# One decoder layer on one core: other PSUM pools, an earlier start of gate/up, read-backs moved into gate/up, and a last quarter in two halves

## The chip, the core and the metric

The kernel runs as one program on one core of a Trainium2 chip. The core has five engines, each with its own in-order instruction queue: TensorE (PE in the rows, its weight loads PEld), VectorE (DVE), ScalarE (ACT), GpSimd (POOL) and SyncE (SP). SP issues nearly all DMA transfers, POOL the accumulating ones. The metric is the time of one execution in microseconds; the kernel before takes 2859.53 us, the median of three runs from 2858.51 to 2861.17.

## What is computed

One layer of a hybrid decoder with 512 tokens and a width of 2048, in float32:

```
u = RMSNorm(h);  p = u @ W_in          # 80 column blocks of 128 for three groups of heads
y = concat(SSD(p), RG_LRU(p), mLSTM(p))  # 2048 + 1024 + 1024 columns
h = h + y @ W_out
g, v = split(RMSNorm(h) @ W_gate_up)   # 2 x 5632 columns
h = h + (silu(g) * v) @ W_down
out = RMSNorm(h)
```

The RG-LRU group (here: LRU) has 8 column blocks. Each block convolves its input over time, multiplies it with two small block-diagonal matrices, takes sigmoids, exponentials and a square root of them, and runs a scan over the tokens.

## The kernel before

Every float32 product with a large weight matrix is made of three fp32r matmuls: both operands are split into a rounded high part and a low part (`hi`, `lo`), and hi x hi, hi x lo and lo x hi are added in PSUM. A weight tile `raw` (128 x 1024) is loaded, ACT copies it to `whi`, DVE subtracts to get `wlo`; three buffers of each are used in turn. Its two halves are the moving operands of 128 x 512 matmuls; the stationary operand is a 128 x 128 piece of an activation tile (`three`, L738 to 743). In the input projection it is the other way round: weights stationary, `u` moving (L144 to 146).

The stages follow each other:

- Input projection with the three groups (L205 to 700). For each block of 128 columns TensorE runs 48 matmuls into a bank `mm` (3 banks), and small matmuls and transposes of the groups, in 5 banks `sm`, are placed between them. `lru(i)` (L429) multiplies the convolved tile `xc` (one buffer) with two matrices into two banks `ps_l` (L447); ACT reads each with a sigmoid (`tr`, `ti`), and a chain on ACT, DVE and POOL ends in a scan and the next block's `xc`. Blocks 6 and 7 come after the last mLSTM head.
- Read-back of the SSD half: `ssd_half` loads 16 tiles `yt`, scales and splits them into `vh`, `vl`.
- Output projection (L728 to 800): the first half of W_out's rows for 4 column blocks, then the second half for 4 column blocks, each 8 weight tiles by 4 token tiles into 4 of 6 banks `ac`. After each block of the second half, h's new tiles `hx` are transposed (`tp`, 2 banks), scaled to `ft` and partly split for gate/up.
- Gate/up (L848 to 920): `seven(j)` for 11 column blocks. It is one step of Strassen's scheme: 7 products ("blocks" 1, 5, 6, 3, 7, 2, 4 in that order) in place of 8, of 48 matmuls each. The weights' sums are made by DMA: `more` issues accumulating transfers on POOL's queue into the tiles `k1` (4 buffers) and `k2` (4). `swiglu` makes the activation, TensorE transposes it, and it is stored to DRAM (`at`).
- Down (L924 to 957): the activations are read back (`ae`), split into a pool of 54 tiles and multiplied with W_down, first the blocks 0 to 5 and then 6 to 10, each for 4 column blocks of 4 token tiles: 88 weight tiles of 24 matmuls, 2112 in all. At the end each of the 4 token tiles is normalised in one DVE instruction of 128 x 2048 and stored.

The order of each engine's instructions is made when the program is built: a scheduler takes the instructions by their place in the code and by when it reckons operands and buffers to be ready, and a pool hands out a buffer when the one before is released. A new PSUM pool without `reuse_waits="tile"` takes the place of the closed pools as a whole; with it, a new tile waits only for the tiles that lay where it lies.

Where tiles lie in a partition of SBUF is fixed at the build, too. The starts of `whi` and `wlo`, of the split activations of the output projection, and of those of gate/up are 224 bytes past a multiple of 256. Those of down's 54 tiles are 96 bytes past one.

Of the kernel before, what the change touches and what calls it, by code (L numbers as in the profile page):

```python
# [15 lines left out]
F32 = mybir.dt.float32  # L16
F32R = mybir.dt.float32r
AF = mybir.ActivationFunctionType
ALU = mybir.AluOpType
# [47 lines left out]
def trunk(tc, A, out):  # L67
# [207 lines left out]
    with tc.tile_pool(name="ssd", bufs=2, side="right", reuse_waits="tile") as sp:  # L275
# [39 lines left out]
        for g in range(NG):  # L315
# [15 lines left out]
            ps = bank("ps_bt")  # L331
# [71 lines left out]
            ps = bank("ps_g")  # L403
# [25 lines left out]
    def lru(i):  # L429
# [315 lines left out]
    def all_tokens(srcs, x):  # L745

        ps = [acc_bank() for _ in range(4)]
        for n, src in enumerate(srcs):
            w = halves(raw_tile(src))
            for j in range(2):  # L750
                for t in range(4):
                    three(ps[t], x(2 * n + j, t), w[j], n + j == 0, n == len(srcs) - 1 and j == 1)
        return ps

    def token_tile(xs):
        return lambda k, t: tuple(v[:, t * P:(t + 1) * P] for v in xs[k])

    with tc.tile_pool(name="wo", bufs=2, reuse_waits="tile") as wo:
# [15 lines left out]

        xs = {}
# [5 lines left out]
        for mb in range(4):  # L781
            cols = slice(mb * T, (mb + 1) * T)
            ps = all_tokens([A["w_out"][1, mb, n] for n in range(8)], token_tile(yb))
            for t in range(4):
# [4 lines left out]
                dve.bn_stats(out=stats[:, t, mb], in_=xt)  # L789
                tp = ps_tp.tile([P, T], F32, name="tp", tag="tp")  # L790
                for d in range(4):
                    pe.transpose(out=tp[:, d * P:(d + 1) * P], in_=xt[:, d * P:(d + 1) * P], identity=ident)
# [4 lines left out]
            if mb < 2:  # L797
                for a in range(2):
# [3 lines left out]
                    put(7, mb, a, s3, vtile)  # L802
    upool_cm.__exit__(None, None, None)
    xpool_cm = tc.tile_pool(name="xpool", bufs=25, reuse_waits="tile")
# [5 lines left out]
    for i in (5, 6, 3):  # L810
        for q in range(2):
            for a in range(2):
                f11, f12, f21, f22 = ft[a, q], ft[a, q + 2], ft[a + 2, q], ft[a + 2, q + 2]
                if i == 5:
                    tt(dve, f21, f22, f21, ALU.subtract)
# [4 lines left out]
                else:  # L820
                    stt(f11, f11, -1.0, f12, ALU.mult, ALU.subtract)
                    put(3, q, a, f11, xtile)
    for i, n in ((2, 0), (4, 2)):
        for q in range(2):
            for a in range(2):

                whole = (i, q, a) != (4, 1, 1)
                put(i, q, a, ft[a + n, q + 2], lambda dt, n, w=whole: (vtile if w or n == "vl" else xtile)(dt, n))
# [25 lines left out]
    with tc.tile_pool(name="gu", bufs=2, reuse_waits="tile") as gu:  # L854
# [5 lines left out]
        def seven(j):  # L860
            def src(quad, n):
                return A["w_gu"][j, quad, n]

            def block(i, ps, tiles, first=True):
                for n in range(4):
                    w = halves(tiles(n))
                    for k in range(2):
                        for a in range(2):
                            d = 2 * (n % 2) + k
                            x = tuple(v[:, d * P:(d + 1) * P] for v in xs[i, n // 2, a])  # L870
                            three(ps[a], x, w[k], first and n + k == 0, n == 3 and k == 1, more=not first)
# [29 lines left out]
            more(s, 1)  # L901
            block(5, b2, lambda n: s[n])
# [150 lines left out]
```

## Time and profile before

| | us |
|---|---|
| median of 3 runs | 2859.53 |
| profiled execution | 2861.73 |
| its span, first to last instruction | 2859.7 |
| TensorE busy | 2750.6 |
| VectorE busy | 1540.5 |
| ScalarE busy | 1089.9 |
| GpSimd busy | 291.5 |

The profiled execution is 2.2 us above the median. The busy time of TensorE counts matmuls that overlap each other once, so it says when TensorE had something in work, and not how fast it worked. The slices of the page are 71.5 us each; PEclk gives the granted clock in tenths, where 9 means full or nearly so.

### The profile page before, as it was taken

How to read it: one execution, taken by the hardware profiler on the slowest of the kernel's cores; microseconds unless marked ns; L12 is line 12 of the kernel's file. 1: busy time of each engine (PE TensorE's matmuls, PEld its weight loads, DVE VectorE, ACT ScalarE, POOL GpSimd, SP SyncE). 2: the span in 40 equal slices, each digit the busy share in tenths (PEclk: the TensorE clock that was granted, in tenths of full speed). 3: DMA queues.
4: the chain of work that ended last, by engine and by line, in shares of the span. 5: the costliest groups of instructions: out<-in, count | busy, mean ns of one | idle time of the engine just before them, and what ended most of it. 6: DMA issues, size and time to landing. Idle time of an engine off the chain costs nothing.

```text
span 2859.7 us, 32183 instructions
## 1 busy us (share of the span) xinstructions
PE 2750.6 (96%) x12566; PEld 2240.9 (78%) x12566; DVE 1540.5 (54%) x2025; ACT 1089.9 (38%) x1305; POOL 291.5 (10%) x321
## 2 busy tenths in 40 slices
PE   8999999999999957999989999999999969999997
PEld 6888888887888836888878888888888858888885
DVE  8766666646776675234465555555555544233233
ACT  4433333323345564212244444444444433122111
POOL 2111111110011100000011111111111100000000
PEclk9999999999999978999999999999999989999998
DMA  4333333223333244443478888888988855233222
GB/s 172 131 111 104 111 103 105 98 96 114 115 118 114 100 153 143 152 155 133 141 191 206 202 201 200 204 201 206 205 202 203 192 183 167 91 118 126 96 89 96
DMA packets 137175, 418.10 MB, mean 146 GB/s; under 512 B 16764, under 2 KB 18844, under 8 KB 135872
## 3 DMA queue, kind: packets, MB, share of 16 engines
q1 hardware_dynamic: 111680, 323.77, 33.7%
q0 software_dynamic: 25344, 92.29, 17.4%
q8 instruction: 98, 1.61, 0.2%
q14 instruction: 53, 0.43, 0.1%
HBM read 377.09 MB, written 32.61 MB: 143 GB/s over the span
## 4 chain that ended last, share of the span: by engine, by line
PE 95%; DVE 2%; DMA 1%; ACT 1%; issue 0%; SPq 0%; DVEq 0%; POOL 0%; ACTq 0%; POOLq 0%
PE ac L742 20%; PE ac L741 20%; PE ac L743 20%; PE mm L144 10%; PE mm L146 10%; PE mm L145 10%; PE tp L887 1%; PE ps_d L385 1%; PE ps_l L447 0%; DMA ae<-at 0%; PE ps_st L359 0%; PE ps_o L390 0%; PE ps_i L631 0%; PE ps_c L640 0%; DMA yt<-y 0%
## 5 line engine op out<-in xcount | busy, mean ns | idle before, releaser
L742 PE MATMUL ac<-wlo,vh 128*128 128x512 f32 x2192 | 861.1, 393 | 2.3 <-DVE wlo L84 2.3
L743 PE MATMUL ac<-whi,vl 128*128 128x512 f32 x2192 | 858.8, 393 | 0.0
L741 PE MATMUL ac<-whi,vh 128*128 128x512 f32 x2192 | 816.0, 394 | 23.1 <-ACT vh L90 17.6
L84 DVE TENSOR_TENSOR wlo<-raw,whi 128x1024 fp32r<-128x1024 f32 x356 | 436.8, 1227 | 625.4 <-ACT whi L90 615.7
L90 ACT ACTIVATE whi<-raw 128x1024 fp32r<-128x1024 f32 x356 | 376.7, 1058 | 1007.1 <-PE ac L743 602.6
L144 PE MATMUL mm<-uh,whi 128*128 128x512 f32 x1280 | 506.1, 395 | 1.3 <-DVE cin L84 0.8
L741 PEld LDWEIGHTS ac<-whi,vh 128*128 128x128 f32 x2192 | 413.4, 189 | 115.3 <-ACT vh L90 18.2
L146 PE MATMUL mm<-uh,wlo 128*128 128x512 f32 x1280 | 503.2, 393 | 0.0
L145 PE MATMUL mm<-ul,whi 128*128 128x512 f32 x1280 | 503.1, 393 | 0.0
L742 PEld LDWEIGHTS ac<-wlo,vh 128*128 128x128 f32 x2192 | 413.4, 189 | 92.6 <-DVE wlo L84 3.0
L84 DVE TENSOR_TENSOR wlo<-k,whi 128x1024 fp32r<-128x1024 f32 x264 | 323.4, 1225 | 300.2 <-ACT whi L90 299.1
L743 PEld LDWEIGHTS ac<-whi,vl 128*128 128x128 f32 x2192 | 413.1, 188 | 90.5
L90 ACT ACTIVATE whi<-k 128x1024 fp32r<-128x1024 f32 x264 | 279.8, 1060 | 318.3 <-PE ac L743 278.3
L144 PEld LDWEIGHTS mm<-uh,whi 128*128 128x128 f32 x1280 | 240.4, 188 | 57.8 <-issue 4.9
L146 PEld LDWEIGHTS mm<-uh,wlo 128*128 128x128 f32 x1280 | 240.4, 188 | 52.8 <-issue 3.0
L145 PEld LDWEIGHTS mm<-ul,whi 128*128 128x128 f32 x1280 | 240.5, 188 | 50.0 <-issue 2.1
L895 POOL DMA_DIRECT2D k<-in_w_gu x176 | 152.4, 866 | 1029.9 <-DVE wlo L84 1019.2
L741 PE MATMUL ac<-whi,uh 128*128 128x512 f32 x256 | 99.9, 390 | 0.0
L742 PE MATMUL ac<-wlo,uh 128*128 128x512 f32 x256 | 99.9, 390 | 0.0
L743 PE MATMUL ac<-whi,ul 128*128 128x512 f32 x256 | 99.0, 389 | 0.0
L87 DVE SCALAR_TENSOR_TENSOR cacc<-cin,half,cacc 128x512 f32<-128x512 f32 x96 | 81.2, 846 | 1.2
L90 ACT ACT_TABLE_LOAD x50 | 64.2, 1283 | 2.3 <-PEq L1045 0.8
(266 smaller groups left out, 1823.4 us busy)
## 6 DMA issues: line engine op xcount, KB each, us to landing
k<-in_w_gu POOLq DMA_DIRECT2D x176, 512.0 KB, 7.2
raw<-in_w_in SPq DMA_DIRECT2D x160, 512.0 KB, 3.6
k<-in_w_gu SPq DMA_DIRECT2D x88, 512.0 KB, 9.7
raw<-in_w_down SPq DMA_DIRECT2D x88, 512.0 KB, 3.3
raw<-in_w_out SPq DMA_DIRECT2D x64, 512.0 KB, 4.2
raw<-in_w_gu SPq DMA_DIRECT2D x44, 512.0 KB, 4.2
at<-e SPq DMA_DIRECT2D x44, 256.0 KB, 5.2
ae<-at SPq DMA_DIRECT2D x44, 256.0 KB, 3.7
```

Source lines behind the costliest of these rows:

```text
L84: eng.tensor_tensor(out=o, in0=a, in1=b, op=op)
L87: dve.scalar_tensor_tensor(out=o, in0=a, scalar=s, in1=b, op0=op0, op1=op1)
L90: act.activation(out=o, in_=a, func=f, **kw)
L144: pe.matmul(ps, lhsT=wh, rhs=xh[:, cols], start=k == 0, stop=False)
L145: pe.matmul(ps, lhsT=wh, rhs=xl[:, cols], start=False, stop=False)
L146: pe.matmul(ps, lhsT=wl, rhs=xh[:, cols], start=False, stop=k == n - 1)
L385: pe.matmul(ps_d[i * 64:(i + 1) * 64, s], lhsT=xd[:, c, i * 64:(i + 1) * 64], rhs=es[i][:, s], start=True, stop=True)
L741: pe.matmul(ps, lhsT=xh, rhs=wh, start=first, stop=False, skip_group_check=more)
L742: pe.matmul(ps, lhsT=xh, rhs=wl, start=False, stop=False, skip_group_check=more)
L743: pe.matmul(ps, lhsT=xl, rhs=wh, start=False, stop=last, skip_group_check=more)
L887: pe.transpose(out=tp[:, f * P:(f + 1) * P], in_=u[:, f * P:(f + 1) * P], identity=ident)
L895: pool.dma_start(out=tiles[n], in_=src(quad, n), accum_op=ALU.add)
```

## The change

Five things change.

- PSUM in the first stages: the pools are `ps_sm` (4 banks), `ps_mm` (3) and a new `ps_l` (1), in this order, and all have `reuse_waits="tile"`, as have the pools `ps_ac` (6) and `ps_tp` (2) that follow. The one bank `ps_l` takes the LRU's two products in turn, and one transpose and one sum of each SSD group.
- Gate/up begins in the output projection: block 1 of column block 0 stands ahead of the transposes of h's last column block, block 2 behind them. For every column block the order of the products is now 1, 2, 5, 6, 3, 7, 4, and the first two `swiglu` stand behind block 3. Some of the activation sums and splits are made in the output projection's last two column blocks; eight tiles of a new pool `extra` hold block 2's.
- In the last `seven`, the activations of blocks 0 to 5 are read back and split into tiles of `extra`, `xpool` and `vpool` as these come free. Down's pool of 54 tiles goes; blocks 6 to 10 go to the same pools.
- Down's last column block of the second half is made for token tiles 0 and 1, and then for 2 and 3, with its 10 weight tiles loaded and split for each.
- The final norm: three quarters of each row are multiplied with the norm's weights on POOL as soon as they are complete, the last quarter after it; then ACT scales one half row and DVE the other, and each half is stored by itself.

With `whi` and `wlo` and the pools that now hold down's activations, all these tiles start 224 bytes past a multiple of 256 in the changed program.

```diff
--- before.py
+++ after.py
...
-    ps_mm_cm = tc.tile_pool(name="ps_mm", bufs=3, space=PSUM)
-    ps_mm = ps_mm_cm.__enter__()
-    ps_sm_cm = tc.tile_pool(name="ps_sm", bufs=5, space=PSUM)
-    ps_sm = ps_sm_cm.__enter__()
+    ps_cm = [tc.tile_pool(name=n, bufs=b, space=PSUM, reuse_waits="tile")
+             for n, b in (("ps_sm", 4), ("ps_mm", 3), ("ps_l", 1))]
+    ps_sm, ps_mm, ps_l = [c.__enter__() for c in ps_cm]
 
     def bank(name):
         return ps_sm.tile([P, T], F32, name=name, tag="sm")
+    def side_bank(name):
+        return ps_l.tile([P, T], F32, name=name, tag="l")
...
-            ps = bank("ps_bt")
+            ps = side_bank("ps_bt")
...
-            ps = bank("ps_g")
+            ps = side_bank("ps_g")
...
-            ps = bank("ps_l")
+            ps = side_bank("ps_l")
...
-    ps_sm_cm.__exit__(None, None, None)
-    ps_mm_cm.__exit__(None, None, None)
-    ps_ac = ctx.enter_context(tc.tile_pool(name="ps_ac", bufs=6, space=PSUM))
-    ps_tp = ctx.enter_context(tc.tile_pool(name="ps_tp", bufs=2, space=PSUM))
+    for c in reversed(ps_cm):
+        c.__exit__(None, None, None)
+    ps_ac = ctx.enter_context(tc.tile_pool(name="ps_ac", bufs=6, space=PSUM, reuse_waits="tile"))
+    ps_tp = ctx.enter_context(tc.tile_pool(name="ps_tp", bufs=2, space=PSUM, reuse_waits="tile"))
+    extra_cm = tc.tile_pool(name="extra", bufs=8, side="right", reuse_waits="tile")
+    extra = extra_cm.__enter__()
+    def etile(dt, name):
+        return extra.tile([P, T], dt, name=name, tag="x2")
...
-    def all_tokens(srcs, x):
-        ps = [acc_bank() for _ in range(4)]
+    def token_rows(srcs, x, ts):
+        ps = {t: acc_bank() for t in ts}
         for n, src in enumerate(srcs):
             w = halves(raw_tile(src))
             for j in range(2):
-                for t in range(4):
+                for t in ts:
                     three(ps[t], x(2 * n + j, t), w[j], n + j == 0, n == len(srcs) - 1 and j == 1)
         return ps
 
+    def all_tokens(srcs, x):
+        return token_rows(srcs, x, range(4))
...
+            hx = []
             for t in range(4):
                 xt = wo.tile([P, T], F32, name="hx", tag="hx", bufs=4)
                 sync.dma_start(out=xt, in_=h_d[t][:, cols])
                 tt(dve, xt, ps[t], xt, ALU.add)
                 sync.dma_start(out=h_d[t][:, cols], in_=xt)
-                dve.bn_stats(out=stats[:, t, mb], in_=xt)
+                if mb < 3:
+                    dve.bn_stats(out=stats[:, t, mb], in_=xt)
+                hx.append(xt)
+            if mb == 3:
+                b1, b3 = ([acc_bank() for _ in range(2)] for _ in range(2))
+                block(1, b1, lambda n: raw_tile(A["w_gu"][0, 0, n]))
...
+            else:
+                for a in range(2):
+                    put(2, mb - 2, a, ft[a, mb], etile)
+                if mb == 3:
+                    block(2, b3, lambda n: raw_tile(A["w_gu"][0, 2, n]))
+                for a in range(2):
+                    f21 = ft[a + 2, mb - 2]
+                    tt(dve, f21, ft[a + 2, mb], f21, ALU.subtract)
+                if mb == 3:
+                    for t in range(4):
+                        dve.bn_stats(out=stats[:, t, mb], in_=hx[t])
...
+        def acts_in(j, make):
+            for t in range(4):
+                e = gu.tile([P, T], F32, name="ae", tag="e", bufs=3)
+                sync.dma_start(out=e, in_=at_d[j][t])
+                acts[j, t] = split_into(e, make)
+        def seven(j, done=None):
...
-            b1, b2, b3 = ([acc_bank() for _ in range(2)] for _ in range(3))
+            b1, b3 = done or [[acc_bank() for _ in range(2)] for _ in range(2)]
+            b2 = [acc_bank() for _ in range(2)]
+            last = j == NB - 1
             s = [wk(src(0, n), "k1") for n in range(4)]
-            block(1, b1, lambda n: s[n])
+            if not done:
+                block(1, b1, lambda n: s[n])
             r1 = save(b1, "r1")
             more(s, 1)
+            if not done:
+                block(2, b3, lambda n: raw_tile(src(2, n)))
+            for a in range(2):
+                tt(dve, r1[a], r1[a], b3[a], ALU.add)
+            if last:
+                acts_in(0, etile)
             block(5, b2, lambda n: s[n])
             r5 = save(b2, "r5")
             v = [wk(src(3, n), "k2") for n in range(4)]
             more(s, 3)
+            if last:
+                acts_in(1, xtile)
             block(6, b1, lambda n: s[n], first=False)
             r2 = save(b1, "r2")
+            if last:
+                acts_in(2, xtile)
             block(3, b2, lambda n: v[n], first=False)
             for a in range(2):
                 tt(dve, r2[a], r2[a], b2[a], ALU.add)
+                swiglu(a, r1[a], r2[a])
...
-            block(2, b3, lambda n: raw_tile(src(2, n)))
-            for a in range(2):
-                tt(dve, r1[a], r1[a], b3[a], ALU.add)
-                swiglu(a, r1[a], r2[a])
...
+            if last:
+                for i in (3, 4, 5):
+                    acts_in(i, vtile)
...
+        acts = {}
+        seven(0, (b1, b3))
+        for j in range(1, NB):
...
-        for js in (range(0, 6), range(6, NB)):
-            acts = {}
-            for j in js:
-                for t in range(4):
-                    e = dn.tile([P, T], F32, name="ae", bufs=3)
-                    sync.dma_start(out=e, in_=at_d[j][t])
-                    acts[j, t] = split_into(e, lambda dt, name: dn.tile([P, T], dt, name=name, tag="a", bufs=54))
...
+        def down(js, mb, ts):
+            cols = slice(mb * T, (mb + 1) * T)
+            ps = token_rows([A["w_down"][mb, n] for n in range(2 * js[0], 2 * js[-1] + 2)], act_of(js), ts)
+            for t in ts:
+                tt(dve, h[t][:, cols], h[t][:, cols], ps[t], ALU.add)
+                if js[-1] == NB - 1:
+                    dve.bn_stats(out=fstats[:, t, mb], in_=h[t][:, cols])
+                    if mb < 3:
+                        tt(pool, h[t][:, cols], h[t][:, cols], nf[:, cols], ALU.mult)
+        def finish(ts):
+            for t in ts:
+                cols = slice(3 * T, 4 * T)
+                fmv = const.tile([P, 1, 2], F32, name=f"fmv{t}")
+                dve.bn_aggr(out=fmv[:, 0], in_=fstats[:, t].rearrange("p a b -> p (a b)"))
+                r = rms(fmv, 1, f"rf{t}")
+                tt(pool, h[t][:, cols], h[t][:, cols], nf[:, cols], ALU.mult)
+                half_row = KD * P // 2
+                actf(h[t][:, 0:half_row], h[t][:, 0:half_row], AF.Copy, scale=r)
+                sync.dma_start(out=out[t][:, 0:half_row], in_=h[t][:, 0:half_row])
+                dve.tensor_scalar(out=h[t][:, half_row:], in0=h[t][:, half_row:], scalar1=r, scalar2=None, op0=ALU.mult)
+                sync.dma_start(out=out[t][:, half_row:], in_=h[t][:, half_row:])
+        js = range(0, 6)
+        for mb in range(4):
+            down(js, mb, range(4))
+        js = range(6, NB)
+        for j, make in zip(js, (vtile, etile, xtile, xtile, vtile)):
+            for t in range(4):
+                e = dn.tile([P, T], F32, name="ae", bufs=3)
+                sync.dma_start(out=e, in_=at_d[j][t])
+                acts[j, t] = split_into(e, make)
+        for mb in range(3):
+            down(js, mb, range(4))
+        for ts in ((0, 1), (2, 3)):
+            down(js, 3, ts)
+            finish(ts)
```

TensorE's rows from the last matmul of the input projection (`mm`) to the first of the output projection (`ac`), in the program before; the numbers tell the LRU's blocks apart (7846 and 7849 are block 5's, 8150 and 8153 block 6's, 8315 and 8318 block 7's):

```order
L146 MATMUL mm_8243<-uh_212,wlo_8253 128x512
L447 MATMUL ps_l_7846<-xc_7773,lbd_7842 128x512
L447 MATMUL ps_l_7849<-xc_7773,lbd_7842 128x512
L447 MATMUL ps_l_8150<-xc_8077,lbd_8146 128x512
L447 MATMUL ps_l_8153<-xc_8077,lbd_8146 128x512
L447 MATMUL ps_l_8315<-xc_8242,lbd_8311 128x512
L447 MATMUL ps_l_8318<-xc_8242,lbd_8311 128x512
L741 MATMUL ac_8351<-whi_8357,vh_7885 128x512
```

The same place in the changed program, with the rows around block 7's two products (8318 and 8321), with 93 and 116 matmuls of the output projection ahead of them:

```order
L149 MATMUL mm_8246<-uh_215,wlo_8256 128x512
L450 MATMUL ps_l_8153<-xc_8080,lbd_8149 128x512
L450 MATMUL ps_l_8156<-xc_8080,lbd_8149 128x512
L749 MATMUL ac_8358<-whi_8364,vh_7888 128x512
...
L751 MATMUL ac_8360<-whi_8454,vl_7944 128x512
L450 MATMUL ps_l_8318<-xc_8245,lbd_8314 128x512
...
L750 MATMUL ac_8360<-wlo_8485,vh_7959 128x512
L450 MATMUL ps_l_8321<-xc_8245,lbd_8314 128x512
L751 MATMUL ac_8360<-whi_8484,vl_7960 128x512
```

Of the six products that stood between the two projections, two are left there; block 5's have moved 153 and 129 rows up into the input projection, and block 7's stand inside the output projection's first column block.

TensorE's rows from the last matmul of the output projection to the first of gate/up, in the program before:

```order
L743 MATMUL ac_10407<-whi_10620,ul_9484 128x512
L792 MATMUL tp_10653<-cmat_72,hx_10648 128x128 x4
L792 MATMUL tp_10665<-cmat_72,hx_10660 128x128 x4
L792 MATMUL tp_10677<-cmat_72,hx_10672 128x128 x4
L792 MATMUL tp_10689<-cmat_72,hx_10684 128x128 x4
L741 MATMUL ac_10821<-whi_10835,vh_9780 128x512
```

The same place in the changed program (`ac_10424` is the output projection's, `ac_10681` gate/up's block 1, `ac_10683` its block 2):

```order
L751 MATMUL ac_10424<-whi_10637,ul_9491 128x512
L749 MATMUL ac_10681<-whi_10687,vh_9787 128x512
...
L820 MATMUL tp_10757<-cmat_75,hx_10665 128x128 x4
L820 MATMUL tp_10764<-cmat_75,hx_10669 128x128 x4
...
L749 MATMUL ac_10683<-whi_10795,vh_10411 128x512
...
L820 MATMUL tp_10771<-cmat_75,hx_10673 128x128 x4
...
L820 MATMUL tp_10778<-cmat_75,hx_10677 128x128 x4
```

26 matmuls of gate/up now stand ahead of the first transposes, and more of them between these and the rest.

SP's rows at the end of gate/up in the program before (`hf` is h for the final sum, `nf` the norm's weights, `ae` the read-back):

```order
L890 DMA at10_10817<-e_16978 128x512
L933 DMA hf0_16987<-h0_7870 128x2048
L933 DMA hf1_16989<-h1_7871 128x2048
L933 DMA hf2_16991<-h2_7872 128x2048
L933 DMA hf3_16993<-h3_7873 128x2048
L936 DMA nf_16995<-in_norm_f 128x2048
L943 DMA ae_16998<-at0_10807 128x512
```

The same stretch in the changed program:

```order
L901 DMA ae_16596<-at0_10962 128x512
...
L925 DMA at10_10972<-e_16890 128x512
...
L901 DMA ae_17110<-at5_10967 128x512
...
L925 DMA at10_10972<-e_17137 128x512
L736 DMA raw_17429<-in_w_down 128x1024
L982 DMA hf0_17144<-h0_7873 128x2048
```

Of the 24 read-backs of blocks 0 to 5, 12 now stand ahead of all stores of block 10, and all 24 ahead of its last two; `hf` and `nf` stand behind them and behind the first 10 weight tiles of down.

## Rows read from the trace of the kernel before

**Rows 1.** The page: span, and the granted clock in 40 slices

```profile
span 2859.7 us, 32183 instructions
...
PEclk9999999999999978999999999999999989999998
```

**Rows 2.** Waits of PE: line, waited for, us in total, times, longest

```profile
PE ps_l L447 <- DVE xc L87: 45.2, 3, 22.6
PE ac L741 <- ACT vh L90: 17.6, 1, 17.6
PE tp L887 <- DVE r L87: 6.4, 3, 2.9
```

**Rows 3.** Windows, PE: us, PE busy (matmuls), granted clock, DMA share, GB/s

```profile
1031.84:1091.66 59.82, 11.48 (x14) 0.56 0.26 83
1091.66:1096.70 5.04, 5.04 (x12) 0.50 0.00 0
1447.71:1465.30 17.59, 10.15 (x33) 0.61 0.98 323
2318.90:2349.40 30.50, 6.44 (x21) 0.55 0.73 277
2840.55:2859.68 19.13, 0.00 (x0) 0.60 0.53 219
```

**Rows 4.** Timeline of PE around the LRU's last products: start, us, instruction, idle before

```profile
1006.27 1.88 PE L447 MATMUL ps_l<-xc,lbd 128*128 128x512 f32 x4
1007.59 0.79 PE L144 MATMUL mm<-uh,whi 128*128 128x512 f32 x1
...
1038.33 3.78 PE L447 MATMUL ps_l<-xc,lbd 128*128 128x512 f32 x4 [6.33 <-DVE xc L87]
1064.67 3.75 PE L447 MATMUL ps_l<-xc,lbd 128*128 128x512 f32 x4 [22.56 <-DVE xc L87]
1084.77 3.78 PE L447 MATMUL ps_l<-xc,lbd 128*128 128x512 f32 x4 [16.35 <-DVE xc L87]
1091.66 0.80 PE L741 MATMUL ac<-whi,vh 128*128 128x512 f32 x1 [3.10 <-ACT ti L90]
```

**Rows 5.** Timeline of ACT: the two reads of the last pair

```profile
1086.88 0.69 ACT L90 ACTIVATE tr<-ps_l,vecs 128x512 f32<-128x512 f32 x1 [2.71 <-PE ps_l L447]
...
1090.92 0.69 ACT L90 ACTIVATE ti<-ps_l,vecs 128x512 f32<-128x512 f32 x1
```

**Rows 6.** Windows, PE: a stretch of the output projection, one of down

```profile
1110.00:1290.00 180.00, 180.00 (x796) 1.00 0.50 167
2400.00:2540.00 140.00, 140.00 (x602) 1.00 0.29 94
```

**Rows 7.** Timeline: PE's first transposes behind the output projection, ACT's first split of down

```profile
1447.71 1.04 PE L792 MATMUL tp<-cmat,hx 128*128 128x128 f32 x8
...
2345.24 1.92 ACT L90 ACTIVATE vh<-ae 128x512 fp32r<-128x512 f32 x3 [16.32 <-DMA ae<-at]
```

**Rows 8.** Timeline of the end: DVE, ACT and SP

```profile
2841.57 0.67 DVE L84 TENSOR_TENSOR hf<-hf,ac 128x512 f32<-128x512 f32 x1
...
2844.14 0.85 ACT L90 ACTIVATE rf<-rf,eps 128x1 f32<-128x1 f32 x4 [18.01 <-DVE rf L84]
...
2844.74 2.33 DVE L87 SCALAR_TENSOR_TENSOR hf<-hf,rf,nf 128x2048 f32<-128x2048 f32 x1
...
2847.10 7.24 SPq L962 DMA_DIRECT2D out_dram<-hf  x4
```

**Rows 9.** The page: splits of weight tiles, and DMA issues

```profile
L84 DVE TENSOR_TENSOR wlo<-raw,whi 128x1024 fp32r<-128x1024 f32 x356 | 436.8, 1227 | 625.4 <-ACT whi L90 615.7
L90 ACT ACTIVATE whi<-raw 128x1024 fp32r<-128x1024 f32 x356 | 376.7, 1058 | 1007.1 <-PE ac L743 602.6
...
raw<-in_w_down SPq DMA_DIRECT2D x88, 512.0 KB, 3.3
```

**Rows 10.** Timeline of POOL: one product of two 128x512 tiles

```profile
1097.68 1.30 POOL L84 TENSOR_TENSOR xc<-xc,tr 128x512 f32<-128x512 f32 x1 [15.57 <-DVE tr L87]
```

More of the change, by code (lines that the diff above doesn't have):

```diff
@@ L750, in all_tokens, with block @@
             for j in range(2):
-                for t in range(4):
+                for t in ts:
                     three(ps[t], x(2 * n + j, t), w[j], n + j == 0, n == len(srcs) - 1 and j == 1)
         return ps
+    def all_tokens(srcs, x):
+        return token_rows(srcs, x, range(4))
     def token_tile(xs):
         return lambda k, t: tuple(v[:, t * P:(t + 1) * P] for v in xs[k])
+    xs = {}
+    def block(i, ps, tiles, first=True):
+        for n in range(4):
+            w = halves(tiles(n))
+            for k in range(2):
+                for a in range(2):
+                    d = 2 * (n % 2) + k
+                    x = tuple(v[:, d * P:(d + 1) * P] for v in xs[i, n // 2, a])
+                    three(ps[a], x, w[k], first and n + k == 0, n == 3 and k == 1, more=not first)
     with tc.tile_pool(name="wo", bufs=2, reuse_waits="tile") as wo:
@@ L802, in trunk @@
                     put(7, mb, a, s3, vtile)
+            else:
[9 more added lines that the diff above has]
+                        dve.bn_stats(out=stats[:, t, mb], in_=hx[t])
     upool_cm.__exit__(None, None, None)
-    xpool_cm = tc.tile_pool(name="xpool", bufs=25, reuse_waits="tile")
+    xpool_cm = tc.tile_pool(name="xpool", bufs=17, reuse_waits="tile")
     xpool = xpool_cm.__enter__()
@@ L821, in trunk @@
                     stt(f11, f11, -1.0, f12, ALU.mult, ALU.subtract)
-                    put(3, q, a, f11, xtile)
-    for i, n in ((2, 0), (4, 2)):
-        for q in range(2):
-            for a in range(2):
-                whole = (i, q, a) != (4, 1, 1)
-                put(i, q, a, ft[a + n, q + 2], lambda dt, n, w=whole: (vtile if w or n == "vl" else xtile)(dt, n))
+                    put(3, q, a, f11, vtile)
+    for q in range(2):
+        for a in range(2):
+            put(4, q, a, ft[a + 2, q + 2], lambda dt, n, w=(q, a) == (1, 1): (xtile if w and n == "vh" else vtile)(dt, n))
     mv = const.tile([P, 4, 2], F32, name="mv")
@@ L858, in wk @@
             return r
-        def seven(j):
+        def acts_in(j, make):
[4 more added lines that the diff above has]
+        def seven(j, done=None):
             def src(quad, n):
                 return A["w_gu"][j, quad, n]
[L864 to L871, printed above, removed]
             def save(ps, name):
@@ L947, in act_of, with f @@
+        def act_of(js):
+            def f(k, t):
                 f = k % 4
                 return tuple(v[:, f * P:(f + 1) * P] for v in acts[js[0] + k // 4, t])
-            for mb in range(4):
-                cols = slice(mb * T, (mb + 1) * T)
-                ps = all_tokens([A["w_down"][mb, n] for n in range(2 * js[0], 2 * js[-1] + 2)], act_of)
-                for t in range(4):
-                    tt(dve, h[t][:, cols], h[t][:, cols], ps[t], ALU.add)
-                    if js[-1] == NB - 1:
-                        dve.bn_stats(out=stats[:, t, mb], in_=h[t][:, cols])
@@ L957, in trunk @@
-        for t in range(4):
-            mv = dn.tile([P, 1, 2], F32, name=f"mv{t}")
-            dve.bn_aggr(out=mv[:, 0], in_=stats[:, t].rearrange("p a b -> p (a b)"))
-            r = rms(mv, 1, f"rf{t}")
-            stt(h[t], h[t], r, nf, ALU.mult, ALU.mult)
-            sync.dma_start(out=out[t], in_=h[t])
+            return f
+        def down(js, mb, ts):
[7 more added lines that the diff above has]
+                        tt(pool, h[t][:, cols], h[t][:, cols], nf[:, cols], ALU.mult)
@@ new lines, in trunk @@
+        js = range(0, 6)
[3 more added lines that the diff above has]
+        for j, make in zip(js, (vtile, etile, xtile, xtile, vtile)):
+            for t in range(4):
+                e = dn.tile([P, T], F32, name="ae", bufs=3)
[6 more added lines that the diff above has]
+            finish(ts)
```

17 lines of the change are left out of this document (7 added, 10 removed).

## Prediction

> **What bounds the kernel now.** The page comes first. TensorE has something in work for 2750.6 of 2859.7 us, and the clock line shows full clock but for four places, near the slices 15, 21, 33 and 40 [rows 1]. So TensorE is the bound nearly everywhere, and there are two ways to save: its idle places with the half clock around them, and the pace of its matmuls. The waits name the idle places: 45.2 us for the LRU's `xc`, 17.6 for down's first split activation, 6.4 for gate/up's last transposes [rows 2]. Windows over the four places give clock and count [rows 3]; the timeline shows what stands in the longest [rows 4]. The last view compares the pace of two stretches of the same function `three` [rows 6].
>
> **The hole ahead of the output projection.** From the last matmul of the input projection to the first of the output projection it is 59.82 us, and the next 5.04 us run at clock 0.50, which loses another 2.5 [rows 3]: 62.3. In it stand three pairs of the LRU's products, each waiting for a chain through ACT, DVE and POOL of 22.56 and 16.35 us from the end of one pair to the next [rows 4]. The output projection could not begin before the last pair was read: its first matmul ended a wait for `ti` [rows 4].
> The order of the changed program takes block 5's pair into the input projection and block 7's into the output projection. A pair that runs in a full stream costs 1.3 us (1006.27 to 1007.59) [rows 4]: 2.6 for two. Block 6's pair stands uncovered, and with one bank its second product waits for the sigmoid that reads the first: 1084.77 to 1087.57, 2.8 us [rows 4, 5], and 0.7 for the second product: 3.5.
> Then the waits for `xc`. Block 5's first product stands 99 matmuls behind block 4's second, block 6's 130 behind block 5's; at 0.226 us each [rows 6] that covers 22.4 and 29.4 us. The chain took 22.56 and 16.35, and 30.2 from block 4 to 5 (1008.15 to 1038.33) [rows 4], where DVE also had the SSD half to split. By the short chains nothing is waited for, by the long one 7.8 and 0.8. I take 1.5, near the short chains, because the splits of the SSD half now stand mainly behind block 5. Block 7's 93 matmuls cover 21.0 us of a 16.35 us chain. Sum: -62.3 + 2.6 + 3.5 + 1.5 = **-54.7**, from -56.2 to -47.6.
>
> **From the output projection to gate/up.** The window is 17.59 us at a clock of 0.61 with 33 matmuls [rows 3]. Sixteen are transposes (8 take 1.04 [rows 7]) and the rest gate/up's, at full clock 2.0 + 17 x 0.226 = 5.8; so 11.8 are lost. In the new order 26 matmuls of block 1, 5.9 us, lie between the last product and the transposes, and the rest of blocks 1 and 2 covers the splits. I keep 0.5: **-11.3**, and -7 if the splits of block 5 still come late by the 4 to 5 us by which the first transposes and splits do now.
>
> **From gate/up to down.** The window is 30.50 us at clock 0.55 with 21 matmuls [rows 3]: 12 transposes (1.4) and 9 of down (2.0), so 27.1 are lost. The longest part is ACT's wait of 16.32 us for the first `ae` [rows 7], behind 5 MB of `hf` and `nf` on SP. The new order reads back before them. What is late next is `ae`'s three buffers, shared with `swiglu`: 24 tiles at 2 us each are 48 us, beside some 65 us that are left of the last `seven`. The bytes are no more than before: 24 x 0.25 MB take the place of the next turn's 12 x 0.5 MB. I keep 1: **-26.1**, and -9.8 if the 16.32 stay.
>
> **The end.** From TensorE's end to the span's end it is 19.13 us [rows 3]. DVE adds and takes statistics until 2844, ACT's four square roots end at 2844.99, then come four products of 2.33 us each, the last store at 2854, and 5.3 us to the end [rows 8]. After the change two token tiles are left. Two adds and two statistics at 0.6 and the small operations give the root at 4.0; POOL's two products of a quarter (1.30 each [rows 10]) end near 4.9; ACT's and DVE's halves by 6.2 at the 1.06 of a 128 x 1024 copy [rows 9]; and the last half row lands 3.3 (a transfer of 0.5 MB [rows 9]) to 5.3 us later: 9.6 to 11.6. I take 11: **-8.1**, between -9.5 and -4 (the halves in turn, not together).
> The price is 10 more weight tiles. Each needs 1.06 on ACT and 1.23 on DVE [rows 9], and 12 matmuls last 2.7: both hide behind TensorE, and a load of 3.3 us hides behind three buffers. Without that cover it would be up to 1 us a tile.
>
> **The pace of down.** In the output projection 796 matmuls take 180 us, 0.2261 each; in down 602 take 140 us, 0.2326 each, at the same clock of 1.00 [rows 6]. The function, the banks and the weight tiles are the same. What differs is where the stationary tiles lie: 96 bytes past a multiple of 256 in down, 224 elsewhere, as the weight tiles do. In the changed program all lie at 224. Down has 2112 matmuls: 2112 x 0.0065 = **-13.7** if the place is the cause, 0 if not. I take -13.7, since I find no other difference.
> The Trainium skill ("SBUF — State Buffer", Who interferes with whom) gives TensorE two independent read ports, for weights and moving operand, and lets only VectorE and GpSimd contend; by that the place costs nothing and this term is 0, the first rival below. The two windows do not bear out that the pace is everywhere the same, but they cannot show why.
>
> **What is unpriced.** One bank less for the groups' small products: in the input projection no wait of PE of over 1 us stands in the trace after the first load, so the sum has nothing for it; the nearest price of a late bank is the 2.8 us read above. Gate/up's new order: block 2 gives the first accumulation of each turn 11 us more, and block 4 still has 22. I put 4 us in the sum for all of these, from 0 to one wait of the LRU's size, 22.56 [rows 4].
>
> **Sum.** -54.7 - 11.3 - 26.1 - 8.1 - 13.7 + 4 = -109.9. Against the profiled 2861.7 that is 2751.8; the median of the runs is 2.2 lower, so **2749.6**. The likeliest case alone lies between 2740 (no new wait, the shortest end) and 2762 (the LRU's 8.6 and a late block 5).
>
> **Rivals.**
> *The pace stays.* For it speaks that nothing in the rows names the place of a tile; against it, that two stages of the same code run at two paces without a wait. Then 2749.6 + 13.7 = 2763.3.
> *The waits move and do not go.* If the LRU's chain stays as slow as 30.2 us, and the read-backs share the DMA with the accumulations so that down still waits 16.3, then 2749.6 + 7.1 + 16.3 = 2773, a little more if the clock falls. Speaks for it: DMA is 0.7 to 1.0 busy around the seams [rows 3]. Against it: the bytes of the last turn are unchanged. That the output projection is not begun early at all would need its banks to be held; the order shows them free after the last `mm` is read.
> *Gate/up starves: slower than before.* Block 2's four `raw` tiles now stand right behind block 1, with three buffers; the fourth is asked for on SP behind stores that wait for `swiglu`. If each of 11 turns waits over 109.9 / 11 = 10.0 us for it, the kernel is slower, at over 2860. A tile whose load was not ahead at all costs 3.3 + 1.06 + 1.23 = 5.6 us [rows 9], so two in each turn would have to come so. Against it: three of four are asked for a whole turn ahead, and PE never waits inside gate/up now [rows 2].
>
> **Chances.** The likeliest 0.71, the pace stays 0.16, the waits move 0.11, slower 0.02. What a measurement of this kernel can tell from no change is about 0.2%, 5.7 us; no case lies there but by chance. Faster 0.97, within 0.2% 0.01, slower 0.02. The range of 8 in 10 reaches from 2738 to 2777: it takes in the first rival and most of the second, and leaves out the third.
>
> **What would show it.** Right: PE's idle of the `ps_l` line falls under 10 us, no half clock between the output projection and down, `ac` matmuls in down at 0.226, some 11 us behind TensorE's end. Wrong: 0.2326 in down; a wait of PE for `xc`, `cin` or `ae` over 5 us; idle TensorE inside gate/up's turns; or new waits on the one bank in the SSD stage.

## The result and the profile after

The changed kernel takes 2770.8 us (median of 4 runs, 2768.9 to 2774.2) against 2860.0: a ratio of 0.969, interval 0.9673 to 0.9707. That is 89 us faster. The forecast was 2749.6, with 2738 to 2777 as the range.

The page of the profiled execution, span and clock in 40 slices, answers to [rows 1]:

```profile
span 2769.6 us, 32286 instructions
...
PEclk9999999999999999999999999999999999999999
```

The waits of PE (line, waited for, total, times, longest) answer to [rows 2]:

```profile
PE ac L749 <- ACT whi L93: 6.6, 2, 5.4
...
PE ps_l L450 <- DVE xc L90: 4.5, 1, 4.5
PE ac L750 <- DVE wlo L87: 1.9, 4, 0.6
```

The windows (us, PE busy and matmuls, granted clock, DMA share, GB/s) are, in turn, the hole between the projections, the 9 matmuls behind it, gate/up's first turn, its last one, the end, and the two stretches of [rows 6]:

```profile
1035.01:1043.60 8.59, 3.31 (x5) 0.73 0.69 229
1043.60:1046.50 2.90, 2.90 (x9) 0.63 0.36 73
1424.02:1433.20 9.18, 3.19 (x7) 0.72 1.05 274
2230.00:2250.00 20.00, 17.65 (x68) 0.93 0.99 213
2756.50:2769.60 13.10, 0.20 (x1) 0.60 0.40 160
1110.00:1290.00 180.00, 180.00 (x804) 1.00 0.48 156
2400.00:2540.00 140.00, 140.00 (x619) 1.00 0.38 122
```

The hole of 59.82 us [rows 3] has become 8.59. Down now does 619 matmuls in 140 us, not 602 [rows 6]. But a window of low clock at full DMA remains at 1424, and the last turn of gate/up has gaps that were not there.

To split the gain I compare matmuls of the same number in the two traces (both hold 12566), and from the output projection on, where the order differs, PE's loss: the time from one start to the next beyond 0.2267 us for a matmul and 0.1085 for a transpose, its usual values. The hole is the first seam between two stages, the passage from the output projection to gate/up the second, that from gate/up to down the third.

```
                                     before   after    gain   forecast
loss up to the last LRU pairs (numbers 1 to 4866)      -2.3    -4.0 (unpriced, all)
hole (matmul 4866 to 5200)           135.34   85.76   +49.6   +54.7
output projection to gate/up, loss    12.4     10.1    +2.3   +11.3
gate/up's turns, loss                  1.3      3.0    -1.7    (in the 4.0)
gate/up to down, loss                 27.5      5.5   +22.0   +26.1
pace of down, loss                    13.9      0.0   +13.9   +13.7
end                                   19.13    12.9    +6.2    +8.1
sum                                                   +90.0  +109.9
```

The spans differ by 90.1, so nothing is left over. The 20 us that are missing are 9 at the second seam, 5 in the hole, 4 at the third seam and 2 at the end. No run took the earlier start of gate/up, the earlier read-backs or the new end by itself; those three gains are read from the two traces alone.

**What is late at the second seam.** ACT's first weight splits of block 5, the first whose tiles are accumulated (start, us, instruction, idle before and what ended it):

```profile
1428.44 1.04 ACT L93 ACTIVATE whi<-k 128x1024 fp32r<-128x1024 f32 x1
...
1432.04 1.06 ACT L93 ACTIVATE whi<-k 128x1024 fp32r<-128x1024 f32 x1 [1.17 <-DMA k<-in_w_gu]
1435.80 1.06 ACT L93 ACTIVATE whi<-k 128x1024 fp32r<-128x1024 f32 x1 [2.70 <-DMA k<-in_w_gu]
1439.19 1.06 ACT L93 ACTIVATE whi<-k 128x1024 fp32r<-128x1024 f32 x1 [2.33 <-DMA k<-in_w_gu]
```

Two things are to be seen. The first split begins without a wait just ahead of it: ten operand splits of later blocks, a table load and the tanh stand ahead of it on ACT. The next three come 3.4 to 3.8 us apart, each ended by the landing of a k tile, while 12 matmuls take 2.7. The chain that ended last names the same places, and the read-backs for the third seam (start, us, what):

```profile
1431.63 10.76 DMA k<-in_w_gu
...
2222.23 7.41 DMA ae<-at
...
2234.81 9.05 DMA ae<-at
```

There ACT waits for `ae` with weight splits queued behind it, 3.37 us at the longest:

```profile
2224.39 0.63 ACT L93 ACTIVATE vh<-ae 128x512 fp32r<-128x512 f32 x1 [2.91 <-DMA ae<-at]
...
2236.62 0.63 ACT L93 ACTIVATE vh<-ae 128x512 fp32r<-128x512 f32 x1 [3.37 <-DMA ae<-at]
```

**The end**, DVE, ACT, POOL and SP in turn, answers to [rows 8]:

```profile
2757.34 1.28 DVE L1001 BATCH_NORM_STATS2 fstats<-hf 128x6 f32<-128x512 f32 x2
...
2761.24 1.42 DVE L1015 TENSOR_SCALAR hf<-hf,rf 128x1024 f32<-128x1024 f32 x2
```

```profile
2760.64 0.48 ACT L93 ACTIVATE rf<-rf,eps 128x1 f32<-128x1 f32 x2 [9.58 <-DVE rf L87]
2761.23 2.19 ACT L93 ACTIVATE hf<-hf,rf 128x1024 f32<-128x1024 f32 x2
```

```profile
2758.11 2.48 POOL L87 TENSOR_TENSOR hf<-hf,nf 128x512 f32<-128x512 f32 x2 [23.57 <-DVE fstats L1001]
```

```profile
2763.76 1.14 SPq L1014 DMA_DIRECT2D out_dram<-hf  x1
```

The halves run side by side as forecast, ACT's until 2763.4, 6.7 us behind TensorE's end at 2756.7 (forecast 6.2). From there to the end it is 6.2 us, more than the 3.3 to 5.3 I had allowed.

### The profile page after: what moved, and what is told of

It is laid out like the page before. It is cut to its first block, busy times and chain, and to the rows that moved or that the text cites. A ratio compares the mean times of both kernels' runs of the same rounds, so it can differ in the third digit from the quotient of the medians.

```text
span 2769.6 us, 32286 instructions
## 1 busy us (share of the span) xinstructions
PE 2733.8 (99%) x12566; PEld 2236.9 (81%) x12566; DVE 1547.0 (56%) x2035; ACT 1104.8 (40%) x1319; POOL 314.5 (11%) x337
## 3 DMA queue, kind: packets, MB, share of 16 engines
q1 hardware_dynamic: 114272, 331.11, 35.8%
q0 software_dynamic: 25344, 92.29, 18.4%
## 4 chain that ended last, share of the span: by engine, by line
PE 97%; DMA 1%; DVE 1%; ACT 0%; issue 0%; ACTq 0%; SPq 0%; DVEq 0%
PE ac L749 20%; PE ac L750 20%; PE ac L751 20%; PE mm L147 11%; PE mm L149 11%; PE mm L148 11%; PE ps_d L388 1%; PE tp L922 1%; DMA ae<-at 1%; PE ps_l L450 1%; DMA k<-in_w_gu 0%; PE ps_i L634 0%; PE ps_st L362 0%; PE ps_o L393 0%; PE ps_c L643 0%; DVE wlo L87 0%
## 5 line engine op out<-in xcount | busy, mean ns | idle before, releaser
L749 PE MATMUL ac<-whi,vh 128*128 128x512 f32 x2192 | 807.7, 391 | 6.6 <-ACT whi L93 6.6
L87 DVE TENSOR_TENSOR wlo<-raw,whi 128x1024 fp32r<-128x1024 f32 x370 | 457.8, 1237 | 608.7 <-ACT whi L93 599.0
L93 ACT ACTIVATE whi<-raw 128x1024 fp32r<-128x1024 f32 x370 | 391.5, 1058 | 942.8 <-PE ac L751 545.0
L87 POOL TENSOR_TENSOR hf<-hf,nf 128x512 f32<-128x512 f32 x16 | 25.1, 1594 | 485.9 <-DVE fstats L1001 485.9
```

What stands on the lines that cost most here:

```text
L87: eng.tensor_tensor(out=o, in0=a, in1=b, op=op)
L93: act.activation(out=o, in_=a, func=f, **kw)
L749: pe.matmul(ps, lhsT=xh, rhs=wh, start=first, stop=False, skip_group_check=more)
```

## The experiments

The theories: (1) the place of down's stationary tiles sets its pace; (2) the bank of its own, not the release tile by tile, opened the hole; (3) at the second seam block 5 is late by the order on ACT and DVE, or by the DMA; (4) at the third seam the waits for `ae` on ACT hold up the weight splits.

**The place alone.** The kernel before, with 128 unused bytes ahead of down's operands:

```
+        pad = dn.tile([P, 32], F32, name="pad")
+        pool.memset(pad, 0.0)
```

> The kernel before with one unused tile of 128 bytes put ahead of down's split activations, so that these stationary tiles start 224 bytes past a multiple of 256, as everywhere else, and not 96; nothing else is changed. If the place sets the pace, down's 2112 matmuls go from 0.2333 us to 0.2267 us from start to start, 13.7 to 14.0 us in all: about 2846 us. If the place does not matter, down stays at 0.2333 and the time at 2860 us.

2848.3 us, ratio 0.9956 (0.9941 to 0.9971), 12.8 us faster. A window in down:

```profile
2420.00:2560.00 140.00, 140.00 (x620) 1.00 0.32 105
```

Matmuls are now 0.2267 us apart in all of down, and 0.2333 before. Theory 1 holds, and the size with it.

**Which place.** Two kernels, run once each: one with buffers 32 bytes longer, one with a tag for each block of rows and pads between them.

```
-                    acts[j, t] = split_into(e, lambda dt, name: dn.tile([P, T], dt, name=name, tag="a", bufs=54))
+                    acts[j, t] = split_into(e, lambda dt, name: dn.tile([P, T + 8], dt, name=name, tag="a", bufs=54)[:, 0:T])
```

> The kernel before, with down's split activations in buffers of 2080 bytes instead of 2048, so that the 54 buffers step by 32 bytes through all eight places modulo 256. If the place sets the pace, matmuls fall into groups by the place of their stationary tile: 0.2267 us from start to start where it is 224, the slow 238 ns at 96 and at some of the other six, and the whole time lies between 2846 and 2860 us. If the place does not matter, every group shows the 0.2333 us of the kernel before. Which of the other six are slow is left to the run.

2858.2 us. There `hi` lies at 32, 96, 160 or 224 and its `lo` 32 bytes further, so no operand has both at one place. By the place of `hi` every group came out between 231 and 234 ns; split further by product they go from 229.6 to 237.2, and none reaches 226.7. That holds, too, for a `hi` at 224 with the weight tiles at 224: 231.3 ns with `whi` and 237.2 with `wlo`.

```
+    STEP = {0: 160, 1: 32, 2: 32, 3: 64, 4: 32, 5: 32}
...
+                    pool.memset(dn.tile([P, STEP[i] // 4], F32, name=f"pad{i}"), 0.0)
...
-                    acts[j, t] = split_into(e, lambda dt, name: dn.tile([P, T], dt, name=name, tag="a", bufs=54))
+                    acts[j, t] = split_into(e, lambda dt, name: dn.tile([P, T], dt, name=name, tag=f"a{i}", bufs=8))
```

> The kernel before, with down's split activations in a pool for each of six blocks of 512 rows, hi and lo of one block at one place, and the six at 0, 32, 64, 128, 160 and 192 modulo 256 (the kernel before had all at 96, the kernel with the pad all at 224). Each weight tile's matmuls then show the pace of one place. If the place by itself sets the pace, some blocks run at 0.2267 us and some at 0.2333, each the same in all eight column passes; if it is only 96 that is slow, all six run at 0.2267. If the pace goes by something else that the pad moved, all run alike.

2860.5 us. Mean time between starts, from the trace, with the two places known before:

```
place mod 256    0     32     64     96    128    160    192    224
ns            233.3  233.4  234.2  233.3  233.3  229.0  233.4  226.7
```

Six places are slow, 160 is between, 224 alone is fast; and 224 is where the moving weight tiles lie. So the next one moves those.

```
+    shift = ctx.enter_context(tc.tile_pool(name="shift", bufs=1))
+    nc.gpsimd.memset(shift.tile([P, 32], F32, name="pad"), 0.0)
     wpool = ctx.enter_context(tc.tile_pool(name="wpool", bufs=1))
```

> The kernel before with an unused tile of 128 bytes ahead of the weight tiles, so that both halves of the weight tiles lie at 96 modulo 256 instead of 224. The stationary tiles then lie at 224 in the SSD half of the output projection and in down, and at 96 in the other half of the output projection. If 224 for the stationary tile is what is fast, down runs at 0.2267 us and the second half of the output projection at 0.2333. If it is that both tiles lie at one place, the second half stays at 0.2267, and the first half and down run at 0.2333. If only 224 for both is fast, all three run slow.

2876.6 us in one run. The windows are the first half of the output projection, the second half and down:

```profile
1110.00:1200.00 90.00, 90.00 (x389) 1.00 0.57 189
...
1380.00:1430.00 50.00, 50.00 (x230) 1.00 0.41 136
2420.00:2560.00 140.00, 140.00 (x604) 1.00 0.29 94
```

In the kernel before these windows hold 398, 230 and 602. The second half, with both tiles at 96, keeps its pace (16 transposes stand in the window in both); the first half, with 224 against 96, has become as slow as down. Gate/up tells the same within one stage: its blocks 5, 6 and 3, whose operands the pad moved to 96 with the weight tiles, run at 226.7 to 227.9 ns, its blocks 1, 7, 2 and 4, left at 224, at 232.4 to 232.9 (226.7 to 227.7 for all seven in the kernel before). So it is fast where the stationary and the weight tiles lie at one place modulo 256, whether 224 or 96, and where `hi` and `lo` both lie there: the kernel with the longer buffers shows that one pair of equal places is not enough. The Trainium skill ("SBUF — State Buffer", Who interferes with whom) calls TensorE's two read ports independent; by that all these paces would be equal. The runs show 6.6 ns a matmul between them, and not by what mechanism.

**Bank or release.** The changed kernel with one half of the PSUM edit undone.

```
-             for n, b in (("ps_sm", 4), ("ps_mm", 3), ("ps_l", 1))]
+             for n, b in (("ps_sm", 5), ("ps_mm", 3))]
```

> The changed kernel with the LRU's products, the beta transposes and the norm sums again in a pool of five banks instead of one bank of their own; the release tile by tile stays. If the bank of its own is what lets the LRU's last pairs stand inside the matmul streams, the three pairs stand together between the two projections again, PE loses some 57 us there instead of 8.3, and the time is 2771 + 49 = 2820 us. If the release tile by tile does it, the output projection begins ahead of the last pair all the same and the time stays under 2790 us.

2813.2 us, 42 above the changed kernel (49 were expected), with the waits of [rows 2] back:

```profile
PE ps_l L450 <- DVE xc L90: 45.2, 3, 22.4
```

```
-    ps_cm = [tc.tile_pool(name=n, bufs=b, space=PSUM, reuse_waits="tile")
+    ps_cm = [tc.tile_pool(name=n, bufs=b, space=PSUM)
...
-    ps_ac = ctx.enter_context(tc.tile_pool(name="ps_ac", bufs=6, space=PSUM, reuse_waits="tile"))
-    ps_tp = ctx.enter_context(tc.tile_pool(name="ps_tp", bufs=2, space=PSUM, reuse_waits="tile"))
+    ps_ac = ctx.enter_context(tc.tile_pool(name="ps_ac", bufs=6, space=PSUM))
+    ps_tp = ctx.enter_context(tc.tile_pool(name="ps_tp", bufs=2, space=PSUM))
```

> The changed kernel without the release tile by tile on the PSUM pools; the bank of its own stays. If the bank alone does it, the time stays within 3 us of 2771 us. If the release tile by tile is needed, the output projection waits until the last pair has been read, one more chain of 16 to 22 us: 2787 to 2793 us.

2772.1 us, ratio 0.9689 (0.9673 to 0.9705): as the changed kernel. The bank did it and the release tile by tile was not needed; theory 2 holds. The likely reason is where the banks lie: the LRU's is the eighth, and the output projection's accumulators take the first six, so neither way of release makes them wait for block 7. With the five common banks the release is worth a little: from matmul 4866 to 5200 it takes 131.6 us there, against 135.3 in the kernel before and 85.8 in the changed one.

**Order or DMA.** First the order: `issue_after` queues the operands of blocks 6, 3 and 4, and the tanh, behind weight splits of the block before.

```
-            block(5, b2, lambda n: s[n])
+            by = block(5, b2, lambda n: s[n])
+            if done:
+                operands(6, by[1])
...
```

> The changed kernel, with the operands of blocks 6, 3 and 4 of gate/up's first turn split behind the second weight tile of the block before each, and the first tanh behind block 3's, on ACT and DVE; in the changed kernel nine of these splits, a table load and the tanh stand on ACT ahead of block 5's first weight split. PE loses 9.7 us there. If the order on ACT and DVE is the cause, most of it goes: 2763 to 2766 us. If the DMA is (ACT waits 1.2 us for the second accumulated k tile, which lands at 1432.0), the first matmuls come earlier and the next ones wait as long: at most 1 us is gained, 2770 us.

2774.8 us, ratio 0.9701 (0.9688 to 0.9715): nothing gained, and PE loses more there (13.8 us, not 10.1). ACT is now free, and waits for each k tile:

```profile
1427.36 1.06 ACT L745 ACTIVATE whi<-k 128x1024 fp32r<-128x1024 f32 x1 [9.25 <-DMA k<-in_w_gu]
1431.22 1.06 ACT L745 ACTIVATE whi<-k 128x1024 fp32r<-128x1024 f32 x1 [2.80 <-DMA k<-in_w_gu]
1434.98 1.06 ACT L745 ACTIVATE whi<-k 128x1024 fp32r<-128x1024 f32 x1 [2.70 <-DMA k<-in_w_gu]
```

The order was in front of the first tile only, by 1 us. Then k2's loads behind the accumulations, without and with that order:

```
+            with tc.issue_after(added):
+                v = [wk(src(3, n), "k2", pool if done else sync) for n in range(4)]
```

> The changed kernel, with the four k2 loads of gate/up's first turn (2 MB) issued on POOL's queue behind the first accumulations instead of on SP ahead of them; one to three of the splits on ACT also fall behind the first weight splits, as the scheduler sees the tiles earlier. If the DMA is the cause of the 9.7 us, 2 MB at some 290 GB/s are 7 us: the k tiles land that much earlier and the time goes to 2764 to 2766 us. If the order on ACT is, at most 2 us are gained, 2769 us. A new wait for k2 in block 3 would show the loads to be late: 3 us or more slower.

> Both edits of the two kernels before together. If the order and the DMA each hold the start of block 5, as the trace reads to me, only this one loses less than 3 us there: 2763 us. If one of them alone is the cause, this one equals the better of the two within 1 us.

2772.1 and 2773.1 us (ratios 0.9693 and 0.9698, intervals 0.968 to 0.9707 and 0.9685 to 0.9712): no gain in either. The first met neither of its expectations; the second equals the better of the two kernels, but only because neither gained. With both edits block 5's k tiles do come every 2.5 to 2.8 us, and then block 6's first one is late:

```profile
1434.66 1.06 ACT L745 ACTIVATE whi<-k 128x1024 fp32r<-128x1024 f32 x1 [0.38 <-DMA k<-in_w_gu]
...
1442.63 1.06 ACT L745 ACTIVATE whi<-k 128x1024 fp32r<-128x1024 f32 x1 [5.86 <-DMA k<-in_w_gu]
```

PE loses 10.1 us in the changed kernel, 13.8, 9.9 and 10.3 in these three. Taking bytes out of one place put them into the next. What is left is to start earlier: with the order of the first of the three kept, k1's loads go on POOL's queue, where they pass SP's raw tiles and stores.

```
-            s = [wk(src(0, n), "k1") for n in range(4)]
+            s = [wk(src(0, n), "k1", pool if done else sync) for n in range(4)]
```

> The kernel with the operands of blocks 6, 3 and 4 split late, and besides the four k1 loads of gate/up's first turn (2 MB) on POOL's queue, where they wait only for the space that the output projection leaves near 1398, instead of on SP behind five raw tiles and four stores (issued at 1412.5). Without the second edit PE loses 4.4 us at block 5's first weight tile and 9.4 behind it. If the late loads are what fills the DMA just when the accumulations need it, both shrink: under 4 us in all, 2763 us. If the DMA's bytes as a whole are the bound, whatever their order, the loss only moves: 2770 us or more.

2768.3 us, ratio 0.9674 (0.9661 to 0.9687): 6.5 us below the kernel with the order alone, with intervals that just do not meet; the 2.5 us to the changed kernel lie inside the intervals. The loads are issued at 1404.6 instead of 1412.5. PE loses 5.8 us there instead of 13.8:

```profile
1405.00:1420.00 15.00, 15.00 (x75) 1.00 0.97 318
1420.00:1428.50 8.50, 8.45 (x37) 1.00 1.06 275
1428.50:1455.00 26.50, 22.72 (x96) 1.00 1.05 256
```

The same stretch in the changed kernel:

```profile
1405.00:1420.00 15.00, 15.00 (x76) 1.00 0.78 277
```

The DMA share there goes from 0.78 to 0.97, so DMA time that was spare is now used, and the clock stays at 1.00 where it fell to 0.72. Behind it the DMA is full in both. Theory 3 is settled for the DMA, and for when its transfers can start: more than half of the loss went with that, and none with the order on ACT and DVE. What holds the 5.8 us that stay is open. The Trainium skill ("DMA: Bandwidth & Descriptors", Issuing engines are not separate DMA queues) says that transfers of all issuing engines run on the same 16 DMA engines, and that issuing from several saves only the time of issuing. These runs agree: k2's loads on POOL's queue gained nothing, and k1's gained where they started earlier.

**The read-backs.**

```
-                e = gu.tile([P, T], F32, name="ae", tag="e", bufs=3)
-                sync.dma_start(out=e, in_=at_d[j][t])
-                acts[j, t] = split_into(e, make)
+                hi, lo = make(F32R, "vh"), make(F32R, "vl")
+                sync.dma_start(out=lo.bitcast(F32), in_=at_d[j][t])
+                acts[j, t] = hi, lo
...
+                with tc.issue_after(by[t][0]), tc.issue_after(by[t][1]):
+                    actf(hi, lo.bitcast(F32), AF.Copy)
...
```

> The changed kernel with down's operands read back straight into the place of their lo half, and each group of four split one block later, one behind each weight tile's split, instead of through three buffers and as soon as they may. In the changed kernel ACT waits five times for ae in the last turn, 11 us in all, with weight splits behind it, and PE loses 5.5 us around 2240. If those waits are the cause, they go and PE loses less than 1.5: 2766.5 us. If the k tiles are late by themselves, since the DMA is full there, the loss stays: 2770.8 us.

2770.3 us, ratio 0.9683 (0.967 to 0.9696). PE loses 2.2 us there, not 5.5, but the time shows no difference. The kernels that leave this place alone lose 2.6 to 5.5 there from one trace to the next, so the edit is not shown to be worth more than that spread. ACT's waits for `ae` are gone, and it waits 4.76 us for a k tile at 2248 instead. Theory 4 is not shown.

**Both together.**

> Both edits that lowered PE's loss at their own place together: block 5's tiles loaded early on POOL's queue with the operands of blocks 6, 3 and 4 split late, and down's operands read back in place with their splits a block later. Alone they took 4.3 us (of 10.1) and 3.3 us (of 5.5) from PE's loss, though the second hardly moved the time. If the two are independent, PE loses about 5.8 and 2.2 us at the two places and the time is 2764 to 2766 us. If the loss at the second place differs from run to run by as much as the edit gave, the time is that of the first alone, 2768 us.

2766.7 us (2765.4 to 2768.5), ratio 0.9668 (0.9655 to 0.9682), the lowest of all. PE loses 7.4 and 2.6 us at the second and the third seam; their windows:

```profile
1424.00:1455.00 31.00, 26.61 (x109) 0.94 1.05 254
2230.00:2250.00 20.00, 19.40 (x84) 1.00 1.07 236
```

4 us below the changed kernel is 0.15%, with overlapping intervals: likely better, not shown.

## Why the prediction was right or wrong

The direction, the order of the three largest terms and the range were right; the likeliest case, 2740 to 2762, was missed by 9 us. Of the signs named for it, PE's wait at `ps_l` (4.5 us), the pace of down (0.2267) and the end (12.9, said were some 11) came about as said. "No half clock between the output projection and down" did not: the granted clock fell to 0.72 for 9 us at the second seam.

- **The hole**, forecast 54.7, measured 49.6, inside its bounds of 47.6 to 56.2. Blocks 5 and 7 run inside the streams, block 6 uncovered, its second product 2.85 us behind the first as forecast (2.8). The chain to block 6 was long, not short: a wait of 4.5, where I took 1.5 out of 0 to 8.6. The reason given for a short chain, that the splits of the SSD half "now stand mainly behind block 5", speaks for a long one: behind block 5 is where block 6's chain runs, and DVE splits the SSD half there, 34 us from block 5's second product to block 6's first.
- **From the output projection to gate/up**, forecast 11.3, measured 2.3, outside even the -7 I kept as the far end. The step that failed is "the rest of blocks 1 and 2 covers the splits. I keep 0.5". The transposes and operand splits are covered to within about 1 us. But I priced only those and not the accumulated k tiles that block 5 needs next: 2 MB of k1, 2 MB of k2, and the accumulations themselves, all asked for from 1412 on behind block 2's tiles. "The bytes are no more than before" was weighed at the other seam; here the change brings the same bytes into less time.
- **From gate/up to down**, forecast 26.1, measured 22.0. The 16.32 us wait is gone. What stayed are 5.5 us in this trace, and 2.6 at the least in a kernel that is alike in this place, so part of the 4 us missed is the spread of one trace. Read-backs and accumulations do share a full DMA there (share 0.99), the rival's condition; that they are the cause is not shown.
- **The pace of down**, forecast 13.7, measured 13.9, and 12.8 by the edit alone: right, though the reason given ("all lie at 224") was half of it. What counts is that they lie where the weight tiles lie, `hi` and `lo` both.
- **The end**, forecast 8.1, measured 6.2, inside its bounds. The last transfer with its completion took longer than allowed. The 10 more weight tiles cost nothing that shows: down loses 0.0.
- **Unpriced**, 4 kept, 4.0 lost: 2.3 up to the last LRU pairs, 1.7 in gate/up's turns. That the two agree is luck, since the 4 was put in without a working. Of the 2.3, 0.6 were lost by the 50th matmul, at a start that differs by some 3 us among these traces, and 1.0 in the last 66 matmuls, where block 5's pair, priced in the hole, now stands. A price of the missing bank is not shown.

By its time the second rival, 2773 with a chance of 0.11, came nearest, in part by luck. Its largest term, 16.3 us of waiting ahead of down, did not come. Its long LRU chain did, for 3 us of its 7.1, and waits did move into the DMA, only at the seam that it did not name. Gate/up did not starve in its turns.

## What to carry to other kernels

When a stall goes, list what the engine needs next, loads included, and when those loads can first be issued; here a full DMA gave a wait back a block later, whatever the order, and only an earlier start helped. A pool's bank count can decide the order of a whole program: one bank apart let two of the last three pairs of products move into the streams. And where two stages of one function run at two paces, compare the places of their tiles.

## What was not expected of the hardware

A matmul of 128 x 512 in this kernel goes at 226.7 ns from start to start where its stationary tiles, `hi` and `lo`, and its weight tiles all begin at the same place modulo 256 bytes (224 and 224, 96 and 96). It goes at 229.0 for 160 against 224, at 232.4 for 224 against 96, and at 233 to 234 for the six other places against 224. With `hi` and `lo` at two places no product was fast, equal pairs included. Accumulating transfers are dear: on the changed kernel's page the queue that mostly accumulates moves 92.29 MB in 18.4% of the engines' time, the other 331.11 MB in 35.8%:

```profile
q1 hardware_dynamic: 114272, 331.11, 35.8%
q0 software_dynamic: 25344, 92.29, 18.4%
```

That is 1.8 times the time for a byte. It is neither the stage nor the queue: from 1500 to 2180 us of the changed kernel, in gate/up, a packet of 4096 bytes takes 202 ns plain and 363 ns accumulating, and on POOL's queue in the kernel with the early loads k1's plain packets take 186 ns, the accumulating ones right behind them 325.
